# 32 affine and 12 weight-splitting operations move from GpSimd to VectorE, and the delta inverse's products skip zero and finished columns

## The chip, the cores and the metric

The kernel runs on one core of a Trainium2 chip. The metric is the device time of one execution in microseconds, as the median of several runs. The engines have short names here: PE is the matrix engine TensorE (PEld its loads of the stationary operand), DVE is VectorE, ACT is ScalarE, POOL is GpSimd, SP is SyncE, which issues most of the DMAs.

## The reference, cut to what matters

Two layers work on 256 latent and 256 context tokens of 1024 columns. Each layer is a SwiGLU FFN, a mixer and another FFN, and each of the three is closed by `x <- LN(alpha*x + gate*f(modulate(x)))`. The layer norm ends in an affine step:

```python
def layer_norm(x, g, b):
    mu = jnp.mean(x32, axis=-1, keepdims=True)
    var = jnp.mean(jnp.square(x32 - mu), axis=-1, keepdims=True)
    return ((x32 - mu) * lax.rsqrt(var + NORM_EPS) * g + b).astype(x.dtype)
```

The first layer's mixer is a windowed attention with 8 heads beside a gated delta rule in two directions with 4 heads, which needs the inverses of triangular matrices (one plus a strictly triangular part) over chunks of tokens. The second layer's mixer is a dense attention with normed and rotated queries and keys.

## The kernel before, in words

All tensors are float32. A product is made of three matmuls on halves: every weight tile of 128 x 1024 is split into a high part `wh` (ACT, L366) and a low part `wl = wr - wh` (DVE, or POOL where `split_w` is given that engine, L368); activations likewise into `ht_hi` (L261, L266) and `ht_lo` (L268). `mm3` (L383 to L386) multiplies high by high, high by low and low by high. Raw weight tiles `wr` have two buffers, and SP loads them in order.

An FFN runs over 22 chunks of 128 hidden columns in three parts (8, 8, 6). A chunk is 48 matmuls into `pgu` (gate and up); `evac` then makes `sg = silu(gate)` on ACT (L431), `sg * up` on DVE (L432), and splits it (L433, L434). `next_fill` hangs other DVE work behind each chunk, four additions of 1024 columns (L169) for the next modulation vector. After a part, the down products `pdn` are added to the residual rows `r` with the gate (L615, L623).

Between two sublayers stands `boundary(sub)`: `norm_tb` normalises four row blocks of 128 tokens, they are transposed, modulated and split as operands of the next sublayer, and `affine_tb` (L323 to L328) multiplies each row block by the norm's `g` (L326) and adds its `b` (L328). The operands don't need that affine step, since modulation contains it; the rows `r` need it before the next down products are added. For sub 3 it is deferred: `mixer_c` calls it in its scores loop at i = 4.

The first mixer (`ab_proj`) runs from about 415 to 500 us of the profile. It projects 13 chunks of 128 columns, with a convolution along tokens on DVE (`cacc`, L908), gates in small operations, and a DMA issued by POOL that stores the rows as `xs`. POOL then makes products of squares `sqT` (L1122). `delta_inverse` (584 to 634) interleaves with the window attention. For each of 8 units (4 tiles of 128 x 128) it forms a transposed `z`, the product `pN` (L1390), copies it to `va` (ACT, L1394), and three times makes a product `pZ` (L1403) and `o = xT - pZ` on DVE (L1408). Diagonal 32 x 32 blocks `xv` come by DMAs that SP and POOL issue (L1377). The window attention keeps POOL with products `qs` (L1290) that follow ACT.

The second mixer (`mixer_c`) projects from 1480 to 1557: products `pct`, statistics `cst`, normed rows `cx` (L1668), rotation (L1677 to L1681), transposes `pcT` (L1707) with their split `kTlo` (L1712). Its scores loop of 19 iterations follows to 1597 (scores `pSc`, maxima L1754, exponentials `cpe`, weights L1759), then down products, the leading chunks of the last FFN (`plead`, `ht_lo` L299), and that FFN.

A scheduler decides the order on each engine from a simulated timeline of its own. The code's order and explicit dependences (`after`) set what it may choose. Each engine then takes its instructions strictly in that order.

Of the kernel before, what the change touches and what calls it, by code (L numbers as in the profile page):

```python
# [10 lines left out]
F32 = mybir.dt.float32  # L11
F32R = mybir.dt.float32r
AF = mybir.ActivationFunctionType
# [19 lines left out]
class Backbone:  # L33
    def __init__(self, ctx, tc, io):
# [10 lines left out]
        self.lat_tags = LAT_TAGS  # L45
        self.turn_at = 0

    def new_ht(self):
# [274 lines left out]
    def affine_tb(self, tb, after):  # L323
        nc = self.nc
        x = self.row_block(tb)
        i = nc.gpsimd.tensor_tensor(out=x, in0=x, in1=self.lnr[:, 0, :], op=ALU.mult)  # L326
        self.after(i, [after])
        nc.gpsimd.tensor_tensor(out=x, in0=x, in1=self.lnr[:, 1, :], op=ALU.add)  # L328

# [68 lines left out]
    def ffn(self, sub, tail, lat_only=False, fill=()):  # L398
# [30 lines left out]
        def evac(c, pts):  # L429
            sg = fp.tile([128, NT], F32, tag="sg", name="sg", bufs=2)  # L430
            nc.scalar.activation(out=sg, in_=pts[0][:, :NT], func=AF.Silu)  # L431
            nc.vector.tensor_tensor(out=sg, in0=sg, in1=pts[1][:, :NT], op=ALU.mult)  # L432
            nc.scalar.activation(out=h_hi[:, c, :], in_=sg, func=AF.Copy)  # L433
            self.evacuated = nc.vector.tensor_tensor(out=h_lo[:, c, :], in0=sg, in1=h_hi[:, c, :].bitcast(F32), op=ALU.subtract)  # L434
            self.next_fill()

        parts = ((0, 8), (8, 16), (16, 22))
# [39 lines left out]
    def lead_weights(self, sub):  # L477
# [4 lines left out]
        for x in range(2):  # L482
# [6 lines left out]
            for y in range(2):  # L489
                hv, lv = self.split_w(t[:, 2 * y:2 * y + 2, :], x == 0, self.nc.gpsimd if x else None)  # L490
                ws += [(hv[:, z, :], lv[:, z, :]) for z in range(2)]
# [145 lines left out]
    def boundary(self, sub, streams=(0, 1), affine=(0, 1)):  # L637
# [6 lines left out]
        def rows(last):  # L644
            self.load_ln(sub)

            def apply():
                for j in affine:
                    for tb in (2 * j, 2 * j + 1):
                        self.affine_tb(tb, last)  # L650

            if sub == 3:
                self.deferred = apply
            else:
                apply()

# [235 lines left out]
    def ab_conv(self, pt, ch, dst, hold=(), aside=()):  # L892
# [7 lines left out]
        for j in (0, 1, 3, 4):  # L900
            o = j - 2
            t0, t1 = max(0, -o), LAT - max(0, o)
            if j in aside:
# [3 lines left out]
                continue  # L907
            nc.vector.scalar_tensor_tensor(  # L908
                out=av[:, :, t0:t1], in0=pv[:, :, t0 + o:t1 + o], scalar=w(j), in1=av[:, :, t0:t1],
# [26 lines left out]
    def ab_proj(self):  # L936
# [20 lines left out]
        def need(n):  # L957
            while len(ws) <= min(n, len(jobs) - 1):
# [5 lines left out]
                if p not in raws:  # L964
                    raws.clear()
                    raws[p] = self.load_w(w[:, :, p:p + 256])
                eng = nc.gpsimd if c0 < 1280 else None
                ws.append(self.split_w(raws[p][:, :, c0 - p:c0 - p + P], bool(ext), eng))
            return ws[min(n, len(jobs) - 1)]
# [25 lines left out]
        self.start_context()  # L995
        for j in range(2):
            nc.gpsimd.dma_start(out=self.xs[:, 2 * j:2 * j + 2], in_=self.rows[j])
        for n in range(4):
# [3 lines left out]
            if n:  # L1002
                k_tok(n - 1)
        self.vt = vt = L.tile([P, 4, 4, P], F32, tag="gate", name="vt", bufs=1)
        project(*need(4))
# [6 lines left out]
        for h in range(4):  # L1012
# [12 lines left out]
            if h == 1:  # L1025
                rows()

        for h in range(4):
# [6 lines left out]
            if h == 0:  # L1035
                q_tok(3)
                V.tensor_scalar(out=ssq, in0=ssq, scalar1=EPS, scalar2=None, op0=ALU.add)
                exps()
            self.ab_gram(h)
        self.ab_pow(self.rq, ssq, -0.5)  # L1040
        V.tensor_scalar(out=self.rq, in0=self.rq, scalar1=float(P) ** -0.5, scalar2=None, op0=ALU.mult)
# [319 lines left out]
    def delta_inverse(self):  # L1361
# [19 lines left out]
        def begin(n):  # L1381
# [4 lines left out]
            bt = cube(bt)  # L1386
            xT, x = (a, bt) if u < 4 else (bt, a)
            pN = self.bank("sc", "pN")
            for tb in range(4):
                nc.tensor.matmul(  # L1390
                    out=pN[:, tb * P:(tb + 1) * P], lhsT=self.AT[u][:, tb, :], rhs=x[:, tb, :], start=True, stop=True
                )
            N = self.tmp("va")
            i = nc.scalar.activation(out=N, in_=pN, func=AF.Copy)  # L1394
            if n == 7:
                self.mark = i
            state[n] = (xT, N, xT)

        def step(n, it):
            xT, N, Z = state[n]  # L1400
            pZ = self.bank("sc", "pZ")
            for tb in range(4):
                nc.tensor.matmul(  # L1403
                    out=pZ[:, tb * P:(tb + 1) * P], lhsT=N[:, tb * P:(tb + 1) * P], rhs=Z[:, tb, :],
                    start=True, stop=True,
                )
            Zn = self.AT[units[n]] if it == 2 else cube(self.tmp("o"))
            V.tensor_tensor(out=Zn, in0=xT, in1=cube(pZ), op=ALU.subtract)  # L1408
            state[n] = (xT, N, Zn)

# [221 lines left out]
    def mixer_c(self):  # L1632
# [53 lines left out]
        def weights(p):  # L1686
            raw = self.load_w(w[:, :, 256 * p:256 * p + 256])
            return [self.split_w(raw[:, 4 * x:4 * x + 4, :], p % 3 > 0, nc.gpsimd if x else None) for x in range(2)]

# [59 lines left out]
        def scores(i):  # L1749
# [8 lines left out]
            V.reciprocal(out=st[:, 3:4], in_=st[:, 2:3])  # L1758
            V.tensor_scalar(out=pe, in0=pe, scalar1=st[:, 3:4], scalar2=None, op0=ALU.mult)  # L1759
            state[i] = pe  # L1760
# [18 lines left out]
        for i in range(19):  # L1779
            if i == 4:  # L1780
                self.deferred()
            for n in (0, 1) if i == 0 else (i + 1,):
# [106 lines left out]
```

## Time and profile before

| | us |
|---|---|
| median of 3 runs | 1825.21 |
| lowest, highest | 1824.44, 1827.54 |
| profiled execution | 1826.35 |
| its span | 1824.6 |

The profile is of one execution. Its mean granted clock of PE is 0.987. A view that groups instructions gives their number, the time they were busy, the mean of one and the idle time just before them with what ended it. The timeline merges neighbours of one kind into a row with a count; the durations of neighbours overlap a little at their ends, so a row's time is a bit less than the sum of its members'. The waits count only time in which an engine stood idle for the named operation. A window lists for each engine the busy time and, in brackets, the instructions that touch it; the clock is the share of full speed granted to PE, and half of it is the lower of the clock's two levels.

### The profile page before, as it was taken

Reading aid. Unit: us, or ns where it says so; the run is one execution under the profiler, and the core shown is the slowest. Engines: PE = TensorE matmul, PEld = TensorE weight load, DVE = VectorE, ACT = ScalarE, POOL = GpSimd, SP = SyncE. Lnnn points to the kernel's source line nnn. Section 1 sums busy time; section 2 is a strip of 40 time slices with the busy share of each in tenths; the row PEclk is TensorE's granted clock in tenths of the full one; section 3 lists DMA queues with packets and bytes.
Section 4 is the critical chain, followed back from the end, with each engine's and each line's share of the span. In section 5 each row is a group of like instructions: output and inputs, shape, how many; then the busy total and the mean of one; then the engine's idle time right before and its main releaser. Section 6 shows DMA issues by size and latency. Waiting matters only on the chain. (4 is left out here: it accounts for less than half of the span.)

```text
span 1824.6 us, 24388 instructions
## 1 busy us (share of the span) xinstructions
PE 1758.4 (96%) x9571; PEld 1484.9 (81%) x9571; DVE 1264.7 (69%) x1912; ACT 672.8 (37%) x1178; POOL 290.7 (16%) x324
## 2 busy tenths in 40 slices
PE   6999999999998999999999999999999999999997
PEld 2978878878787888877887888778878888878997
DVE  2774855867688986896673438976747769786556
ACT  2432331324664662332221323423332335634442
POOL 1000000017433210510000003400000046150000
PEclk8999999999998999999999999999999999999999
DMA  9563553522341213375552242664644433136552
GB/s 349 185 216 128 185 182 120 197 59 95 127 116 54 75 59 104 128 240 187 162 184 70 93 154 77 212 204 141 204 163 139 155 108 113 59 126 232 186 177 99
DMA packets 178173, 267.56 MB, mean 147 GB/s; under 512 B 14639, under 2 KB 126683, under 8 KB 177547
## 3 DMA queue, kind: packets, MB, share of 16 engines
q1 hardware_dynamic: 172944, 250.58, 41.4%
q0 software_dynamic: 4624, 14.29, 2.4%
q8 instruction: 75, 1.23, 0.3%
q10 hardware_dynamic: 491, 1.15, 0.2%
q14 instruction: 39, 0.32, 0.1%
HBM read 259.64 MB, written 6.34 MB: 146 GB/s over the span
## 5 line engine op out<-in xcount | busy, mean ns | idle before, releaser
L366 ACT ACTIVATE wh<-wr 128x1024 fp32r<-128x1024 f32 (+1 forms) x311 | 324.8, 1056 | 756.7 <-PE pdn L386 306.6
L368 DVE TENSOR_TENSOR wl<-wr,wh 128x1024 fp32r<-128x1024 f32 (+1 forms) x299 | 390.0, 1315 | 231.9 <-ACT wh L366 228.5
L383 PE MATMUL pgu<-ht_hi,wh 128*128 128x512 f32 (+1 forms) x1472 | 519.5, 355 | 14.7 <-DVE sg L432 8.4
L386 PE MATMUL pgu<-ht_hi,wl 128*128 128x512 f32 (+1 forms) x1472 | 520.4, 354 | 3.3 <-DVE wl L368 3.3
L385 PE MATMUL pgu<-ht_lo,wh 128*128 128x512 f32 (+1 forms) x1472 | 520.6, 355 | 1.0 <-POOL ht_lo L268 0.5
L383 PEld LDWEIGHTS pgu<-ht_hi,wh 128*128 128x128 f32 x1472 | 279.1, 191 | 57.8 <-DVE sg L432 10.9
L386 PEld LDWEIGHTS pgu<-ht_hi,wl 128*128 128x128 f32 x1472 | 280.4, 191 | 41.6 <-DVE wl L368 3.9
L385 PEld LDWEIGHTS pgu<-ht_lo,wh 128*128 128x128 f32 x1472 | 280.5, 191 | 39.1 <-POOL ht_lo L268 0.9
L169 DVE SCALAR_TENSOR_TENSOR acc<-wa,cv,acc 128x1024 f32<-128x1024 f32 x224 | 277.1, 1299 | 0.0
L385 PE MATMUL pdn<-wl,hhi 128*128 128x512 f32 (+1 forms) x622 | 241.1, 388 | 0.0
L383 PE MATMUL pdn<-wh,hhi 128*128 128x512 f32 (+1 forms) x622 | 239.9, 389 | 0.0
L386 PE MATMUL pdn<-wh,hlo 128*128 128x512 f32 (+1 forms) x622 | 239.6, 388 | 0.0
L383 PEld LDWEIGHTS pdn<-wh,hhi 128*128 128x128 f32 x622 | 116.7, 188 | 27.6 <-issue 2.5
L385 PEld LDWEIGHTS pdn<-wl,hhi 128*128 128x128 f32 x622 | 116.9, 188 | 23.7
L386 PEld LDWEIGHTS pdn<-wh,hlo 128*128 128x128 f32 x622 | 116.9, 188 | 23.6
L432 DVE TENSOR_TENSOR sg<-sg,pgu 128x512 f32<-128x512 f32 (+1 forms) x86 | 53.6, 623 | 108.6 <-PE pgu L386 105.1
L615 DVE SCALAR_TENSOR_TENSOR tm<-pdn,gate 128x512 f32<-128x512 f32 (+1 forms) x98 | 64.3, 675 | 60.0 <-PE pdn L386 59.8
L197 POOL DMA_DIRECT2D gsc<-rows x12 | 6.2, 525 | 615.3 <-DVE rows L180 615.3
L433 ACT ACTIVATE hhi<-sg 128x512 fp32r<-128x512 f32 (+1 forms) x86 | 49.7, 577 | 89.4 <-DVE sg L432 89.3
L431 ACT ACTIVATE sg<-pgu 128x512 f32<-128x512 f32 (+1 forms) x86 | 45.9, 534 | 59.6 <-PE pgu L386 59.6
L434 DVE TENSOR_TENSOR hlo<-sg,hhi 128x512 fp32r<-128x512 f32 (+1 forms) x86 | 59.8, 695 | 7.7 <-ACT hhi L433 7.7
L318 POOL TENSOR_TENSOR mv<-mv,mhalf 128x1 f32<-128x1 f32 x18 | 16.6, 932 | 272.3 <-DVE mv L317 272.3
(385 smaller groups left out, 2351.3 us busy)
## 6 DMA issues: line engine op xcount, KB each, us to landing
wr<-in_ffn_w_gu_dram SPq DMA_DIRECT2D x84, 1024.0 KB
wa<-in_ada_w_dram SPq DMA_DIRECT2D x144, 512.0 KB
wr<-in_ffn_w_down_dram SPq DMA_DIRECT2D x40, 1024.0 KB
wr<-in_ab_w_in_dram SPq DMA_DIRECT2D x11, 1024.0 KB
wr<-in_c_w_in_dram SPq DMA_DIRECT2D x6, 1024.0 KB
gate<-gsc POOLq DMA_DIRECT2D x10, 512.0 KB, 4.5
wr<-in_ffn_w_gu_dram SPq DMA_DIRECT2D x8, 512.0 KB
wr<-in_ffn_w_down_dram SPq DMA_DIRECT2D x8, 512.0 KB
```

The source lines that it names most:

```text
L169: i = nc.vector.scalar_tensor_tensor(out=acc[:, sl], in0=wa[:, sl], scalar=cv, in1=acc[:, sl], op0=ALU.mult, op1=ALU.add)
L318: nc.gpsimd.tensor_tensor(out=mv[:, 3:4], in0=mv[:, 2:3], in1=self.mhalf[:, 0:1], op=ALU.pow)
L366: self.last_high = nc.scalar.activation(out=hv, in_=raw, func=AF.Copy)
L368: self.last_split = (eng or nc.vector).tensor_tensor(out=lv, in0=raw, in1=hv.bitcast(F32), op=ALU.subtract)
L383: self.first_mm = nc.tensor.matmul(out=out, lhsT=lhs[0], rhs=rhs[0], start=start, stop=False)
L385: self.link(nc.tensor.matmul(out=out, lhsT=lhs[0], rhs=rhs[1], start=False, stop=False))
L386: self.last_mm = nc.tensor.matmul(out=out, lhsT=lhs[1], rhs=rhs[0], start=False, stop=stop)
L431: nc.scalar.activation(out=sg, in_=pts[0][:, :NT], func=AF.Silu)
L432: nc.vector.tensor_tensor(out=sg, in0=sg, in1=pts[1][:, :NT], op=ALU.mult)
L433: nc.scalar.activation(out=h_hi[:, c, :], in_=sg, func=AF.Copy)
L434: self.evacuated = nc.vector.tensor_tensor(out=h_lo[:, c, :], in0=sg, in1=h_hi[:, c, :].bitcast(F32), op=ALU.subtract)
L615: i = nc.vector.scalar_tensor_tensor(out=tm, in0=pt[:, cs], scalar=mul, in1=self.gate[:, t // 2, ds], op0=ALU.mult, op1=ALU.mult)
```

## The change

1. Affine steps. `affine_tb` no longer issues anything. It puts a multiplication and an addition per row block on a list, and `next_affine` takes them from it one by one and issues them on DVE: two after the evacuation of chunks 2 to 5 of an FFN's first part, two behind the convolution of each of the four query heads in `ab_proj`, one in each of the iterations 2 to 5 of `mixer_c`'s scores loop. These are 8 + 8 operations ahead of FFNs two and three, 8 in `ab_proj`, 4 in the scores loop and 4 in the last FFN's leading chunks. The DMA that stores `xs` moves behind the affine operations of heads 1 and 3.
2. Splits. The 12 weight splits that `split_w` gave to POOL go to DVE: four of `ab_proj`, six of `mixer_c`, two of the last FFN's leading weights.
3. The inverse. Its matrices are triangular in blocks of 32 columns. `pN` is made for 96 instead of 128 columns, and of the three `pZ` the first has 96, the second 64 and the third 32. The subtraction covers these columns only and writes straight into `AT`. For each unit POOL gets a memset of the 32 columns of `va` that were not computed and a copy of 32 finished columns into `AT`.
4. `vt` is allocated after the first call of `ab_gram`.

```diff
     def affine_tb(self, tb, after):
         nc = self.nc
         x = self.row_block(tb)
-        i = nc.gpsimd.tensor_tensor(out=x, in0=x, in1=self.lnr[:, 0, :], op=ALU.mult)
-        self.after(i, [after])
-        nc.gpsimd.tensor_tensor(out=x, in0=x, in1=self.lnr[:, 1, :], op=ALU.add)
+        lnr = self.lnr
+
+        self.affine += [
+            lambda i=i: nc.vector.tensor_tensor(out=x, in0=x, in1=lnr[:, i, :], op=(ALU.mult, ALU.add)[i]) for i in range(2)
+        ]
+
+    def next_affine(self, n, behind):
+
+        for _ in range(min(n, len(self.affine))):
+            self.after(self.affine.pop(0)(), [behind])
...
             self.next_fill()
+            if n == 0 and c > 1:
+                self.next_affine(2, self.evacuated)
...
-                hv, lv = self.split_w(t[:, 2 * y:2 * y + 2, :], x == 0, self.nc.gpsimd if x else None)
+                hv, lv = self.split_w(t[:, 2 * y:2 * y + 2, :], x == 0)
...
-                eng = nc.gpsimd if c0 < 1280 else None
-                ws.append(self.split_w(raws[p][:, :, c0 - p:c0 - p + P], bool(ext), eng))
+                ws.append(self.split_w(raws[p][:, :, c0 - p:c0 - p + P], bool(ext)))
...
-        for j in range(2):
-            nc.gpsimd.dma_start(out=self.xs[:, 2 * j:2 * j + 2], in_=self.rows[j])
...
+            self.next_affine(2, self.convolved)
+            if h % 2:
+                nc.gpsimd.dma_start(out=self.xs[:, h - 1:h + 1], in_=self.rows[h // 2])
...
+            c0 = 0 if u < 4 else 32
             pN = self.bank("sc", "pN")
+            p3 = pN[:, 0:384].rearrange("p (t x) -> p t x", t=4)
             for tb in range(4):
                 nc.tensor.matmul(
-                    out=pN[:, tb * P:(tb + 1) * P], lhsT=self.AT[u][:, tb, :], rhs=x[:, tb, :], start=True, stop=True
-                )
-            N = self.tmp("va")
-            i = nc.scalar.activation(out=N, in_=pN, func=AF.Copy)
+                    out=p3[:, tb, :], lhsT=self.AT[u][:, tb, :], rhs=x[:, tb, c0:c0 + 96], start=True, stop=True
+                )
+
+            N = cube(self.tmp("va"))
+            i = nc.scalar.activation(out=N[:, :, c0:c0 + 96], in_=p3, func=AF.Copy)
+            zc = 96 if u < 4 else 0
+            nc.gpsimd.memset(N[:, :, zc:zc + 32], 0.0)
...
+            dc = 0 if u < 4 else 96
+            nc.gpsimd.tensor_copy(out=self.AT[u][:, :, dc:dc + 32], in_=xT[:, :, dc:dc + 32])
+            state[n] = (xT, N)
 
         def step(n, it):
-            xT, N, Z = state[n]
+
+            u = units[n]
+            xT, N = state[n]
+            w = 96 - 32 * it
+            c0 = 128 - w if u < 4 else 0
+            Z = xT if it == 0 else self.AT[u]
             pZ = self.bank("sc", "pZ")
+            p3 = pZ[:, 0:4 * w].rearrange("p (t x) -> p t x", t=4)
             for tb in range(4):
                 nc.tensor.matmul(
...
-            Zn = self.AT[units[n]] if it == 2 else cube(self.tmp("o"))
-            V.tensor_tensor(out=Zn, in0=xT, in1=cube(pZ), op=ALU.subtract)
-            state[n] = (xT, N, Zn)
+                    out=p3[:, tb, :], lhsT=N[:, tb, :], rhs=Z[:, tb, c0:c0 + w], start=True, stop=True,
+                )
+            V.tensor_tensor(
+                out=self.AT[u][:, :, c0:c0 + w], in0=xT[:, :, c0:c0 + w], in1=p3, op=ALU.subtract
+            )
...
-            return [self.split_w(raw[:, 4 * x:4 * x + 4, :], p % 3 > 0, nc.gpsimd if x else None) for x in range(2)]
+            return [self.split_w(raw[:, 4 * x:4 * x + 4, :], p % 3 > 0) for x in range(2)]
...
-            if i == 4:
-                self.deferred()
+            if 1 < i < 6:
+                self.next_affine(1, self.weighted)
```

How the order on the engines changes is shown at three places. In the changed kernel the lines are some 8 to 20 higher: L326 and L328 become L330, L368 L376, L432 L440, L434 L442, L169 L170, L615 L625, L623 L633, L1664 L1683, L1668 L1687, L1677 L1696, L1680 and L1681 L1699 and L1700, L1290 L1295, L1377 L1382, L1403 L1423.

First, DVE in the first part of the second FFN (third and fourth chunk); `acc` is the modulation vector, `r_6318` the latent rows. Before:

```order
L368 TENSOR_TENSOR wl<-wr,wh 128x1024 x2
L434 TENSOR_TENSOR hlo<-sg,hhi 128x512
L169 SCALAR_TENSOR_TENSOR acc_6923<-wa,cv,acc_6923 128x1024 x2
L169 SCALAR_TENSOR_TENSOR acc_6924<-wa,cv,acc_6924 128x1024 x2
L432 TENSOR_TENSOR sg<-sg,pgu_7108 128x512
L368 TENSOR_TENSOR wl<-wr,wh 128x1024
L434 TENSOR_TENSOR hlo<-sg,hhi 128x512
L169 SCALAR_TENSOR_TENSOR acc_6923<-wa,cv,acc_6923 128x1024 x2
```

and now:

```order
L376 TENSOR_TENSOR wl<-wr,wh 128x1024 x2
L330 TENSOR_TENSOR r_6318<-r_6318,lnr 128x1024
L442 TENSOR_TENSOR hlo<-sg,hhi 128x512
L170 SCALAR_TENSOR_TENSOR acc_6915<-wa,cv,acc_6915 128x1024 x2
L170 SCALAR_TENSOR_TENSOR acc_6916<-wa,cv,acc_6916 128x1024 x2
L330 TENSOR_TENSOR r_6318<-r_6318,lnr 128x1024
L440 TENSOR_TENSOR sg<-sg,pgu_7104 128x512
L376 TENSOR_TENSOR wl<-wr,wh 128x1024 x2
```

An affine operation now stands behind the two splits of a chunk, and a second one behind the additions, ahead of the next `sg`.

Second, DVE at the start of the second mixer, between the last additions to the rows and the first rotated `cx`. Before:

```order
L368 TENSOR_TENSOR wl<-wr,wh 128x1024
L623 TENSOR_TENSOR r_6319<-r_6319,tm 128x512 x2
L615 SCALAR_TENSOR_TENSOR tm<-pdn_11790,gate 128x512
L615 SCALAR_TENSOR_TENSOR tm<-pdn_11791,gate 128x512
L623 TENSOR_TENSOR r_6319<-r_6319,tm 128x512 x2
L1664 TENSOR_SCALAR cst<-cst 128x2
L1668 TENSOR_TENSOR cx<-pct,cst 128x256
L1677 TENSOR_TENSOR ct<-cx,tabc 128x256 x2
L368 TENSOR_TENSOR wl<-wr,wh 128x1024
L1680 TENSOR_TENSOR cx<-ct 128x2x64
L1681 TENSOR_TENSOR cx<-ct 128x2x64
```

and now:

```order
L376 TENSOR_TENSOR wl<-wr,wh 128x1024
L633 TENSOR_TENSOR r_6319<-r_6319,tm 128x512 x2
L376 TENSOR_TENSOR wl<-wr,wh 128x1024
L625 SCALAR_TENSOR_TENSOR tm<-pdn_11790,gate 128x512
L625 SCALAR_TENSOR_TENSOR tm<-pdn_11791,gate 128x512
L633 TENSOR_TENSOR r_6319<-r_6319,tm 128x512 x2
L1683 TENSOR_SCALAR cst<-cst 128x2
L1687 TENSOR_TENSOR cx<-pct,cst 128x256
L1696 TENSOR_TENSOR ct<-cx,tabc 128x256 x2
L376 TENSOR_TENSOR wl<-wr,wh 128x1024
L1699 TENSOR_TENSOR cx<-ct 128x2x64
L1700 TENSOR_TENSOR cx<-ct 128x2x64
```

A second split stands between the additions to the rows (and one more ahead of this piece), where POOL made it before; the rotation's own order is unchanged.

Third, POOL in the inverse. `qs` are products of the window attention, `xv` the diagonal blocks, `va` the copy of `pN`. Before:

```order
L1368 MEMSET xv 128x2048
L1290 TENSOR_TENSOR qs<-qTa,qs 64x128 x3
L1377 DMA xv<-scr_in 32x4x32 x8
L1290 TENSOR_TENSOR qs<-qTa,qs 64x128 x3
L1377 DMA xv<-scr_in 32x4x32 x2
L1290 TENSOR_TENSOR qs<-qTa,qs 64x128 x3
```

and now:

```order
L1373 MEMSET xv 128x2048
L1405 MEMSET va 128x4x32
L1295 TENSOR_TENSOR qs<-qTa,qs 64x128 x3
L1382 DMA xv<-scr_in 32x4x32 x8
L1295 TENSOR_TENSOR qs<-qTa,qs 64x128 x3
L1410 COPY AT<-xv 128x4x32
L1405 MEMSET va 128x4x32
L1382 DMA xv<-scr_in 32x4x32
L1410 COPY AT<-z 128x4x32
L1382 DMA xv<-scr_in 32x4x32
```

The memsets of `va` and the copies into `AT` stand among the `qs` and the issues of `xv` DMAs.

## Rows read from the trace of the kernel before

**Rows 1.** The page's shares: busy us, share of the span, instructions of each engine
```profile
PE 1758.4 (96%) x9571; PEld 1484.9 (81%) x9571; DVE 1264.7 (69%) x1912; ACT 672.8 (37%) x1178; POOL 290.7 (16%) x324
```

**Rows 2.** Groups of POOL: line, operation, shapes, count, busy us, mean ns, idle before
```profile
L328 POOL TENSOR_TENSOR r<-r,lnr 128x1024 f32<-128x1024 f32 x16 | 46.9, 2947 | 0.0
L326 POOL TENSOR_TENSOR r<-r,lnr 128x1024 f32<-128x1024 f32 x16 | 42.9, 2709 | 0.0
L368 POOL TENSOR_TENSOR wl<-wr,wh 128x1024 fp32r<-128x1024 f32 x12 | 29.9, 2497 | 11.5 <-ACT wh L366 11.5
```

**Rows 3.** Timeline of POOL behind the first mixer: start, us, operation, count
```profile
759.68 11.68 POOL L326 TENSOR_TENSOR r<-r,lnr 128x1024 f32<-128x1024 f32 x4
```

**Rows 4.** Timeline of DVE there, beside POOL and after it
```profile
762.34 10.10 DVE L368 TENSOR_TENSOR wl<-wr,wh 128x1024 fp32r<-128x1024 f32 x3
772.97 2.81 DVE L368 TENSOR_TENSOR wl<-wr,wh 128x1024 fp32r<-128x1024 f32 x1
...
806.35 2.36 DVE L368 TENSOR_TENSOR wl<-wr,wh 128x1024 fp32r<-128x1024 f32 x2
809.23 4.87 DVE L169 SCALAR_TENSOR_TENSOR acc<-wa,cv,acc 128x1024 f32<-128x1024 f32 x4
```

**Rows 5.** Waits of PE, 740 to 1210: us in total, times, longest
```profile
PE pgu L383 <- DVE sg L432: 8.4, 6, 2.0
```

**Rows 6.** Windows: length, busy us of PE, PEld, DVE, ACT, POOL, clock, DMA share, GB/s
```profile
440.00:485.00 45.00, 40.74 (x205) 31.74 (x204) 35.88 (x68) 28.03 (x87) 28.98 (x15) 0.96 0.34 117
584.00:634.00 50.00, 48.81 (x399) 45.07 (x399) 43.24 (x132) 30.22 (x99) 14.76 (x31) 0.94 0.22 69
800.00:820.00 20.00, 18.13 (x76) 14.54 (x76) 20.00 (x21) 7.08 (x9) 0.00 (x0) 0.95 0.76 254
...
880.00:890.00 10.00, 10.00 (x46) 8.29 (x45) 7.70 (x11) 2.12 (x2) 0.00 (x0) 1.00 0.27 94
...
1510.00:1540.00 30.00, 29.46 (x221) 28.32 (x220) 26.69 (x71) 17.26 (x53) 16.99 (x16) 0.91 0.41 141
1557.00:1580.00 23.00, 21.74 (x146) 18.58 (x145) 19.85 (x71) 18.32 (x55) 0.00 (x0) 1.00 0.07 24
```

**Rows 7.** Timeline of DVE at the second mixer's start
```profile
1492.63 2.51 DVE L268 TENSOR_TENSOR ht_lo<-h,ht_hi 128x256 fp32r<-128x256 f32 x1
...
1497.46 3.21 DVE L368 TENSOR_TENSOR wl<-wr,wh 128x1024 fp32r<-128x1024 f32 x1
...
1505.65 2.46 DVE L1677 TENSOR_TENSOR ct<-cx,tabc 128x256 f32<-128x256 f32 x2
...
1539.19 1.29 DVE L1677 TENSOR_TENSOR ct<-cx,tabc 128x256 f32<-128x256 f32 x2
```

**Rows 8.** Waits of PE, 1500 to 1560
```profile
PE pcT L1707 <- DVE cx L1681: 3.6, 1, 3.6
PE pcT L1707 <- DVE kTlo L1712: 2.0, 1, 2.0
```

**Rows 9.** Waits of PE, 1600 to 1660
```profile
PE pgu L386 <- DVE wl L368: 3.1, 2, 2.3
```

**Rows 10.** Timeline of DVE at the last FFN's start; in brackets idle time before
```profile
1629.86 10.02 DVE L368 TENSOR_TENSOR wl<-wr,wh 128x1024 fp32r<-128x1024 f32 x3
...
1648.14 1.23 DVE L368 TENSOR_TENSOR wl<-wr,wh 128x1024 fp32r<-128x1024 f32 x1 [5.22 <-ACT wh L366]
```

**Rows 11.** Timeline of PE: the inverse, and two passes of 32 moving columns
```profile
608.55 1.06 PE L1390 MATMUL pN<-z,AT 128*128 128x128 f32 x8
609.44 0.38 PE L1324 MATMUL pP<-ident,pexp 128*128 128x128 f32 x2
...
477.73 0.39 PE L859 MATMUL pgc<-gg,ones 128*128 128x32 f32 x2
```

**Rows 12.** Groups of lines in the inverse's stretch, 584 to 634
```profile
L1408 DVE TENSOR_TENSOR o<-xv,pZ 128x512 f32<-128x512 f32 x8 | 5.5, 683 | 3.1 <-PE pZ L1403 2.9
...
L1290 POOL TENSOR_TENSOR qs<-qTa,qs 64x128 fp32r<-64x128 f32 x20 | 9.2, 462 | 27.5 <-ACT qs L1289 27.2
```

More of the change, by code (lines that the diff above doesn't have):

```diff
@@ L46, in __init__ @@
         self.turn_at = 0
+        self.affine = []
     def new_ht(self):
@@ L645, in rows @@
             self.load_ln(sub)
[L647 to L655, printed above, removed]
+            for j in affine:
+                for tb in (2 * j, 2 * j + 1):
+                    self.affine_tb(tb, last)
         def context():
@@ L907, in ab_conv @@
                 continue
-            nc.vector.scalar_tensor_tensor(
+            self.convolved = nc.vector.scalar_tensor_tensor(
                 out=av[:, :, t0:t1], in0=pv[:, :, t0 + o:t1 + o], scalar=w(j), in1=av[:, :, t0:t1],
@@ L1003, in ab_proj @@
                 k_tok(n - 1)
-        self.vt = vt = L.tile([P, 4, 4, P], F32, tag="gate", name="vt", bufs=1)
         project(*need(4))
@@ L1039, in ab_proj @@
             self.ab_gram(h)
+            if h == 0:
+                self.vt = L.tile([P, 4, 4, P], F32, tag="gate", name="vt", bufs=1)
         self.ab_pow(self.rq, ssq, -0.5)
@@ L1387, in begin @@
             xT, x = (a, bt) if u < 4 else (bt, a)
+            c0 = 0 if u < 4 else 32
             pN = self.bank("sc", "pN")
+            p3 = pN[:, 0:384].rearrange("p (t x) -> p t x", t=4)
             for tb in range(4):
                 nc.tensor.matmul(
-                    out=pN[:, tb * P:(tb + 1) * P], lhsT=self.AT[u][:, tb, :], rhs=x[:, tb, :], start=True, stop=True
+                    out=p3[:, tb, :], lhsT=self.AT[u][:, tb, :], rhs=x[:, tb, c0:c0 + 96], start=True, stop=True
                 )
-            N = self.tmp("va")
-            i = nc.scalar.activation(out=N, in_=pN, func=AF.Copy)
+            N = cube(self.tmp("va"))
+            i = nc.scalar.activation(out=N[:, :, c0:c0 + 96], in_=p3, func=AF.Copy)
+            zc = 96 if u < 4 else 0
+            nc.gpsimd.memset(N[:, :, zc:zc + 32], 0.0)
             if n == 7:
                 self.mark = i
-            state[n] = (xT, N, xT)
+            dc = 0 if u < 4 else 96
+            nc.gpsimd.tensor_copy(out=self.AT[u][:, :, dc:dc + 32], in_=xT[:, :, dc:dc + 32])
+            state[n] = (xT, N)
         def step(n, it):
-            xT, N, Z = state[n]
+            u = units[n]
[3 more added lines that the diff above has]
+            Z = xT if it == 0 else self.AT[u]
             pZ = self.bank("sc", "pZ")
+            p3 = pZ[:, 0:4 * w].rearrange("p (t x) -> p t x", t=4)
             for tb in range(4):
                 nc.tensor.matmul(
-                    out=pZ[:, tb * P:(tb + 1) * P], lhsT=N[:, tb * P:(tb + 1) * P], rhs=Z[:, tb, :],
-                    start=True, stop=True,
-                )
-            Zn = self.AT[units[n]] if it == 2 else cube(self.tmp("o"))
-            V.tensor_tensor(out=Zn, in0=xT, in1=cube(pZ), op=ALU.subtract)
-            state[n] = (xT, N, Zn)
+                    out=p3[:, tb, :], lhsT=N[:, tb, :], rhs=Z[:, tb, c0:c0 + w], start=True, stop=True,
+                )
+            V.tensor_tensor(
+                out=self.AT[u][:, :, c0:c0 + w], in0=xT[:, :, c0:c0 + w], in1=p3, op=ALU.subtract
+            )
         jobs = []
@@ L1758, in scores @@
             V.reciprocal(out=st[:, 3:4], in_=st[:, 2:3])
-            V.tensor_scalar(out=pe, in0=pe, scalar1=st[:, 3:4], scalar2=None, op0=ALU.mult)
+            self.weighted = V.tensor_scalar(out=pe, in0=pe, scalar1=st[:, 3:4], scalar2=None, op0=ALU.mult)
             state[i] = pe
```

## The prediction

> **What bounds the kernel now.** I read the shares of the engines first: PE is busy 1758.4 of 1824.6 us, 96%, DVE 69%, POOL 16% [rows 1]. So the end is set by PE's work, plus 66 us in which PE stands still, plus what PE loses while its clock is granted low. A change of POOL and DVE work can win only there, and it loses wherever DVE comes later than PE.
>
> Second, POOL's operations of 1024 columns [rows 2]: 32 affine operations, 16 of 2.95 us and 16 of 2.71, and 12 splits of weights of 2.50: 46.9 + 42.9 + 29.9 = 119.7 us.
>
> Third, what stands beside them. At 759.68 POOL begins eight affine operations, the first four taking 11.68 us [rows 3]. At 762.34 DVE begins three splits that take 10.10 us, 3.37 each, and a fourth at 772.97 takes 2.81. Later, with POOL idle, two splits take 2.36 us and four additions of L169 4.87 [rows 4]. I take 1.2 us as the price of a 1024-column operation on an undisturbed DVE. So the two engines slow each other down: three splits cost DVE 10.10 us instead of 3.5.
>
> Fourth, where PE waits. Behind the two boundaries ahead of the second and third FFN it waits six times for `sg` (L432), 8.4 us [rows 5]. Around the second mixer's projections it waits 3.6 us for `cx` and 2.0 us for `kTlo` [rows 8], and ahead of the last FFN 3.1 us for `wl` [rows 9].
>
> **The change, part by part.** All sums are against the profiled execution: span 1824.6 plus 1.75 around it, 1826.35 us, which lies 1.1 above the median 1825.21. DVE takes on 44 operations of 1.2 us, 53 us in all. What that costs depends on the stage.
>
> *Boundaries ahead of the second and third FFN.* At each, eight affine operations leave POOL. DVE gets back 10.10 - 3.5 = 6.6 us on three splits and 2.81 - 1.2 = 1.6 on the fourth [rows 4], 8.2 us before the third chunk. It takes on 8 x 1.2 = 9.6 us, two operations in each of chunks 2 to 5. Such a chunk is sg 0.7, two splits 2.4, hlo 0.7 (bounded by a split of twice its columns), four additions 4.9 [rows 4], 8.6 us, and with two affine operations 11.0 by full durations; with the overlap that the starts show (two splits in 2.36) nearer to 10.6. PE needs 48 matmuls: 46 touch the 10 us from 880 to 890, so about (10 + 0.4)/46 = 0.226 us each and 10.8 a chunk [rows 6]. DVE is then full, but in four chunks only, and without a backlog from before them. In the kernel before it is the backlog that makes sg late: in 800 to 820 DVE is busy all 20.00 us, PE 18.13 [rows 6]. I expect the waits to go, 4.2 us at each boundary. At 800 to 820 the clock is also 0.95, 0.05 x 20 = 1 us. I take -5 for the first boundary (ends -2 and -5.2) and -3.5 for the second (-1 and -4.2), which leaves a little for the full chunks.
>
> *First mixer's projections (440 to 485).* Eight affine operations (9.6 us) and four splits (4.8) come to DVE, which has 45.00 - 35.88 = 9.1 us free [rows 6]. 14.4 against 9.1: if nothing is given back, 5.3 us stick out. Some of DVE's 35.88 is slowed by POOL, busy 28.98 us there; if that gives back 5.3, the cost is nothing. Ends 0 and +5.3; I take +1.5, nearer to nothing, since the boundaries show what POOL's company costs DVE [rows 4]. The store of `xs`, a DMA that POOL issues, comes later and now waits for DVE's last affine operation; behind it in POOL's queue stand rq and the products of squares (L1122). They would be late if DVE reached that operation only after 485, so I cost the move at nothing with +1 as its upper end, inside the +5.3.
>
> *The inverse's columns (584 to 634).* Moving columns fall from 128 to 96 in pN, and to 96, 64 and 32 in the three products pZ. A group of eight passes begins at 608.55 and the next stretch of work at 609.44: 0.89/8 = 0.111 us for 128 moving columns. Two passes with 32 moving columns and the same stationary size take 0.39 together [rows 11]; as one alone lasts about 0.28 (1.06 less seven pitches), their pitch is 0.11 as well. So the pitch doesn't follow the moving columns here, and PE gains nothing from fewer. DVE's 24 subtractions (0.683 us for 512 columns [rows 12]) lose a quarter, a half and three quarters of their columns: at most 8 x 0.683 x 1.5 = 8.2 us, off the path except where PE waits. PE idles 50.00 - 48.81 = 1.2 us in this stretch [rows 6], which bounds that gain. POOL gets a memset and a copy for each of 8 units, at some 0.46 us (the nearest row, L1290 [rows 12]) 7.4 us in a stretch where it is busy 14.76 of 50: hidden, but for the case of rival C. I take -1, ends -1.2 and +2.
>
> The Trainium skill, "TensorE: Matmul & The Clock Gate", section "LDWEIGHTS (loading the stationary operand)", says that loading the stationary operand takes time by its own columns, about P/1.2 ns: an estimate of 107 ns for 128. By that rule fewer moving columns gain nothing and the sum stands; the trace's 0.111 us agrees. The page's section "Back-to-back issue gap" has the gap of an isolated matmul fall with its moving columns; by that the sum would be rival A's.
>
> *Start of the second mixer.* At 1492.63 an ht_lo of 256 columns takes 2.51 us, at 1497.46 a split 3.21, and at 1505.65 two L1677 take 2.46, which at 1539.19 take 1.29 [rows 7]. DVE wins at least 1.3 + 2.0 + 1.2 = 4.5 us; two more splits ahead of the first L1664 take 2.4 of it. So `cx` comes 2.1 to 2.5 us earlier, of a wait of 3.6 [rows 8]. Behind that gap the clock is 0.91 in 1510 to 1540, 0.09 x 30 = 2.7 us [rows 6]; I count 1. Together -3.5, ends 0 and -6.3. The 2.0 us for `kTlo` go with the POOL work beside them: -2, ends 0 and -2.
>
> *Scores loop (1557 to 1597).* Four affine operations, 4.8 us, go where DVE is busy 19.85 and PE 21.74 of 23.00 us [rows 6]. DVE's free 3.15 us lie in small pieces. Ends 0 and +4.8; I take +2.5.
>
> *Lead and last FFN.* Three splits at 1629.86 took 10.02 us beside POOL; alone they take 3.5. PE's 3.1 us for `wl` should go [rows 9]. The four affine operations stand where DVE had a hole of 5.22 us ahead of 1648.14 [rows 10], so I cost them at nothing; should the hole close, they would cost up to 4.8 of DVE. -3, ends +1 and -6.
>
> **The sum:** -5 - 3.5 + 1.5 - 1 - 3.5 - 2 + 2.5 - 3 = -14.0. 1826.35 - 14.0 = 1812.35, and on the scale of the median, 1.1 less, 1811.
>
> **Rivals.** *A: PE's time follows the columns in the inverse.* 64 passes of pN lose 32 columns each, 64 of each pZ lose 32, 64 and 96: 64 x 224 = 14,336 columns at 0.111/128 us are 12.4 us. For it: no row shows a long run of passes with 32 to 96 columns. Against it: the pair with 32 [rows 11]. It gives 1799. Chance 0.10.
>
> *B: DVE takes POOL's place and the gains are given back.* The boundaries give -1 each because a full DVE leaves no room, the mixer's start 0, kTlo -2, the lead -3, the inverse 0, while the first mixer and the scores loop cost +5.3 and +4.8: +3.1, that is 1828; with half of those two costs, 1823. For it: DVE's 35.88 of 45 and 19.85 of 23 us [rows 6]. Against it: POOL's drag on DVE, 8.2 us at a boundary, is nearly as large as the work that moves, 9.6. Chance 0.13, nearly all of it within 0.2%.
>
> *C: slower, by POOL's queue in the inverse.* The first pZ of a unit now waits for POOL's memset of `va`, and in that queue stand qs (L1290), which waits for ACT 27.2 us over 20 operations, 1.4 each [rows 12], and the issues of xv. If each of the eight units pays one such wait, a qs, a copy and a memset, 1.4 + 3 x 0.46 = 2.8, then 22 us are on the path and the end is 1833. It decides from 18 us on, 2.2 a unit. For it: all of these stand in one queue, one behind the other. Against it: POOL is mostly idle there, and other products lie between. Chance 0.07.
>
> **How the numbers follow.** Forecast 0.70, A 0.10, B 0.13, C 0.07. About 0.2%, 3.65 us, is what a measurement of this kernel can tell: faster means under 1821.6, slower over 1828.9. Forecast and A are faster, 0.80; B the same, 0.13; C slower, 0.07. All better ends together give -24.9, all worse ones +10.1, and they won't all meet. Down I take two thirds of the 10.9 us between, 1811 - 7 = 1804, and 1801 for part of A. Up I take half of the 24.1, 1823, which holds the lower part of B; the worse ends of the first mixer and the scores loop need a DVE that gets nothing back, and those of the boundaries one that does.
>
> **What would show it.** Right: DVE's splits at 1.2 us all along, no wait for sg behind the boundaries, pZ passes still 0.11 us apart, the scores loop 2 to 3 us longer. Wrong: PE waiting for sg or the convolution from a DVE without gaps, pZ passes closer than 0.11 us, or PE waiting for `va` from POOL.

## The result and the profile after

The changed kernel takes 1802.35 us (median of 4 runs, 1800.41 to 1803.31) against 1825.97 for the kernel before: a ratio of 0.9869, 95% interval 0.9852 to 0.9886, 23.6 us faster. The forecast was 1811 within 1801 to 1823. The span fell from 1824.6 to 1800.3. The page's shares, as in [rows 1]:

```profile
PE 1757.1 (98%) x9571; PEld 1481.2 (82%) x9571; DVE 1239.4 (69%) x1956; ACT 670.4 (37%) x1176; POOL 180.5 (10%) x296
```

PE does the same work in 1.3 us less and now fills 98% of the span; POOL lost 110 us of work, and DVE, which took 44 operations on, is busy for 25 us less than before. Two groups of lines on DVE show part of it (line, operation, shapes, count, busy us, mean ns, idle before):

```profile
L376 DVE TENSOR_TENSOR wl<-wr,wh 128x1024 fp32r<-128x1024 f32 x310 | 375.3, 1222 | 220.8 <-ACT wh L374 217.3
...
L330 DVE TENSOR_TENSOR r<-r,lnr 128x1024 f32<-128x1024 f32 x32 | 39.0, 1218 | 0.0
```

The splits now take 1222 ns in the mean, the slowest 1228 (the 298 of before had a mean of 1319 and took up to 3.4 us), so 12 more of them cost 14 us less in total; the affine operations take 1218 ns each and add 39 us. The rest comes from other lines that also lost POOL's company, the splits of activations above all (`ht_lo` L268 from 31.9 to 21.3 us, `hlo` L434 from 51.3 to 45.2), and from the inverse's subtractions, which have fewer columns (16.4 to 10.0).

Where the time went is read from the start of the same instruction on DVE in both timelines, after less before, at the ends of six stages. The same was done for each experiment; the table has the change within a stage, in us, for the profiled execution.

| kernel | to the first mixer's last `tm` (744) | first boundary, to chunk 8 (897) | second FFN, second boundary, to chunk 8 (1272) | to the first score (1559) | scores, to the lead (1621) | last FFN (1798) | sum |
|---|---|---|---|---|---|---|---|
| changed | -0.8 | -6.8 | -2.7 | -5.9 | +1.2 | -9.3 | -24.3 |
| changed again | -2.6 | -6.8 | -2.7 | -6.1 | +1.2 | -9.5 | -26.5 |
| e1, affine only | +7.3 | -2.1 | -2.7 | -2.8 | +1.3 | -5.5 | -4.5 |
| e2, splits only | +3.7 | +1.5 | 0.0 | +1.9 | -0.1 | 0.0 | +7.0 |
| e3, inverse only | +3.0 | -2.0 | 0.0 | +0.1 | +1.9 | +0.5 | +3.5 |
| e4, affine on POOL | +7.4 | -0.1 | +3.7 | -7.1 | +2.8 | -1.5 | +5.2 |
| e5, no affine | -3.5 | -4.8 | -5.4 | -6.1 | -0.1 | -9.3 | -29.2 |
| e6, late in the scores | -2.0 | -6.7 | -2.7 | -6.2 | +0.6 | -9.2 | -26.2 |
| e7, last FFN only | +0.2 | 0.0 | 0.0 | 0.0 | 0.0 | -8.1 | -7.9 |
| e8, without the inverse | -0.3 | -2.3 | -2.7 | -6.2 | +1.2 | -8.3 | -18.6 |
| e9, boundaries only | +0.3 | -4.8 | -2.7 | -0.3 | -0.1 | +0.8 | -6.8 |
| e10, second mixer only | +0.1 | 0.0 | 0.0 | -7.6 | +1.4 | +4.0 | -2.1 |
| e11, first mixer only | 0.0 | +4.2 | 0.0 | +0.1 | -0.1 | +1.6 | +5.8 |

One execution of a kernel differs from the next: the two rows of the changed kernel by 2 us, mostly ahead of 744, and the 12 to 23 times of the kernel before on one chip by 7 to 9 us from lowest to highest. The table has one execution of each, against the profiled execution of the kernel before, so its sums differ from the medians below by up to 3.5 us. The executions of e1, e2, e3, e9, e10 and e11 in it lie 1 to 3 us above their medians.

**The first boundary.** DVE's timeline in the changed kernel, one full chunk (as [rows 4]), and its window (length, busy us of PE, PEld, DVE, ACT, POOL, clock, DMA share, GB/s; as in [rows 6]):

```profile
803.77 0.68 DVE L440 TENSOR_TENSOR sg<-sg,pgu 128x512 f32<-128x512 f32 x1
804.37 2.35 DVE L376 TENSOR_TENSOR wl<-wr,wh 128x1024 fp32r<-128x1024 f32 x2
806.64 1.22 DVE L330 TENSOR_TENSOR r<-r,lnr 128x1024 f32<-128x1024 f32 x1
807.77 0.69 DVE L442 TENSOR_TENSOR hlo<-sg,hhi 128x512 fp32r<-128x512 f32 x1
808.38 4.87 DVE L170 SCALAR_TENSOR_TENSOR acc<-wa,cv,acc 128x1024 f32<-128x1024 f32 x4
813.16 1.22 DVE L330 TENSOR_TENSOR r<-r,lnr 128x1024 f32<-128x1024 f32 x1
814.29 0.68 DVE L440 TENSOR_TENSOR sg<-sg,pgu 128x512 f32<-128x512 f32 x1
```

```profile
800.00:820.00 20.00, 20.00 (x90) 16.57 (x89) 20.00 (x20) 6.49 (x8) 0.00 (x0) 1.00 0.64 213
```

Splits, affine operations and additions follow each other at 1.13 to 1.2 us. From one `sg` (803.77) to the next (814.29) are 10.52 us, and DVE has no gap, but PE has none either. Where it waited 8.4 us for `sg` over both boundaries [rows 5], there is now no such wait.

**The last FFN.** Timeline of DVE and windows (to be read beside [rows 10]):

```profile
1612.60 3.50 DVE L376 TENSOR_TENSOR wl<-wr,wh 128x1024 fp32r<-128x1024 f32 x3 [0.39 <-ACT wh L374]
...
1621.45 1.22 DVE L330 TENSOR_TENSOR r<-r,lnr 128x1024 f32<-128x1024 f32 x1
```

```profile
1620.00:1640.00 20.00, 15.86 (x83) 12.59 (x81) 17.29 (x19) 8.52 (x16) 14.35 (x10) 0.91 0.12 38
1640.00:1665.00 25.00, 22.34 (x178) 21.54 (x179) 12.02 (x17) 10.10 (x15) 0.00 (x0) 1.00 0.73 245
```

```profile
1605.00:1620.00 15.00, 14.81 (x92) 12.29 (x91) 9.52 (x20) 8.92 (x17) 1.81 (x4) 1.00 0.23 70
1620.00:1641.00 21.00, 20.88 (x175) 20.68 (x174) 16.29 (x20) 10.52 (x15) 0.58 (x1) 1.00 0.73 246
```

The first pair of windows is the kernel before, the second the changed one. Before, PE stood still for 4.1 and 2.7 us there, and its clock was 0.91 in the first of them; now for 0.2 and 0.1, at full clock.

**The inverse.** Timeline of PE (as [rows 11]):

```profile
612.92 1.02 PE L1423 MATMUL pZ<-z,va 128*128 128x96 f32 x8
613.78 1.03 PE L1423 MATMUL pZ<-AT,va 128*128 128x64 f32 x8
614.65 0.39 PE L1329 MATMUL pP<-ident,pexp 128*128 128x128 f32 x2
...
615.90 1.00 PE L1423 MATMUL pZ<-AT,va 128*128 128x64 f32 x8
616.73 0.39 PE L1329 MATMUL pP<-ident,pexp 128*128 128x128 f32 x2
616.96 0.98 PE L1423 MATMUL pZ<-AT,va 128*128 128x32 f32 x8
617.77 0.71 PE L1303 MATMUL pS<-kk,qs 128*128 128x512 f32 x2
```

Eight passes of 96 moving columns take 0.86 us to the next start, of 64 columns 0.83 (615.90 to 616.73), of 32 columns 0.81 (616.96 to 617.77), and before 0.89 for 128: 0.108, 0.104 and 0.101 us a pass against 0.111.

### The profile page after: what moved, and what is told of

Same layout as the page of the kernel before. It is cut to its first block, busy times and chain, and to the rows that moved or that the text cites. A ratio compares the mean times of both kernels' runs of the same rounds, so it can differ in the third digit from the quotient of the medians.

```text
span 1800.3 us, 24410 instructions
## 1 busy us (share of the span) xinstructions
PE 1757.1 (98%) x9571; PEld 1481.2 (82%) x9571; DVE 1239.4 (69%) x1956; ACT 670.4 (37%) x1176; POOL 180.5 (10%) x296
## 5 line engine op out<-in xcount | busy, mean ns | idle before, releaser
L376 DVE TENSOR_TENSOR wl<-wr,wh 128x1024 fp32r<-128x1024 f32 (+1 forms) x311 | 375.5, 1219 | 220.8 <-ACT wh L374 217.3
L170 DVE SCALAR_TENSOR_TENSOR acc<-wa,cv,acc 128x1024 f32<-128x1024 f32 x224 | 272.8, 1279 | 0.0
L440 DVE TENSOR_TENSOR sg<-sg,pgu 128x512 f32<-128x512 f32 (+1 forms) x86 | 53.6, 623 | 109.0 <-PE pgu L394 105.0
L625 DVE SCALAR_TENSOR_TENSOR tm<-pdn,gate 128x512 f32<-128x512 f32 (+1 forms) x98 | 64.3, 675 | 61.2 <-PE pdn L394 61.1
L442 DVE TENSOR_TENSOR hlo<-sg,hhi 128x512 fp32r<-128x512 f32 (+1 forms) x86 | 53.6, 624 | 12.2 <-ACT hhi L441 12.2
L394 PE MATMUL pproj<-ht_hi,wl 128*128 128x512 f32 (+1 forms) x160 | 56.1, 355 | 0.0
```

Source lines behind the costliest of these rows:

```text
L170: i = nc.vector.scalar_tensor_tensor(out=acc[:, sl], in0=wa[:, sl], scalar=cv, in1=acc[:, sl], op0=ALU.mult, op1=ALU.add)
L376: self.last_split = (eng or nc.vector).tensor_tensor(out=lv, in0=raw, in1=hv.bitcast(F32), op=ALU.subtract)
L394: self.last_mm = nc.tensor.matmul(out=out, lhsT=lhs[1], rhs=rhs[0], start=False, stop=stop)
L625: i = nc.vector.scalar_tensor_tensor(out=tm, in0=pt[:, cs], scalar=mul, in1=self.gate[:, t // 2, ds], op0=ALU.mult, op1=ALU.mult)
```

## The experiments

The first four take the change apart by its parts.

**e1_affine_only**: the changed kernel with the inverse of before and with the 12 splits back on POOL.

```diff
-                hv, lv = self.split_w(t[:, 2 * y:2 * y + 2, :], x == 0)
+                hv, lv = self.split_w(t[:, 2 * y:2 * y + 2, :], x == 0, self.nc.gpsimd if x else None)
```

> The affine steps go to VectorE at the places of the changed kernel; the 12 splits stay on GpSimd and the inverse stays as before. Theory (the gain is GpSimd's affine work no longer slowing VectorE): the changed kernel gained 6.7 us at the first boundary, 2.7 at the second, 9.4 around the last FFN's start and lost about 2 in the scores loop; all of that belongs to the affine steps, and about half of the 5.9 at the second mixer. So -18 to -21 against the kernel before, near 1806. Rival (the gain is shared evenly by the three parts, or comes from the inverse): -8 to -12, near 1816.

Measured: 1819.37 against 1827.39, ratio 0.9951 (0.9935 to 0.9967), -8.0 us. The theory missed; the figure is the lower end of the rival's -8 to -12, but not for the rival's reason. The table puts the miss in the first mixer, where it is 7.3 us later. The waits of PE (580 to 640) and of ACT (560 to 592) in this run:

```profile
PE pS L1304 <- POOL qs L1296: 8.0, 1, 8.0
```

```profile
ACT qs L1295 <- DVE X L1182: 7.1, 1, 7.1
```

The chain: PE waits 8.0 us for `qs`, which waits for ACT, which waits for the last step of a serial solve on DVE (`X`). DVE's first operation on the gram matrices ahead of that solve came 7.0 us later than before and the last one 6.0 later. In the changed kernel the first came 3.3 later, but the last 0.5 earlier, and the solve began 0.5 earlier: there the rows of gram matrices themselves make up the delay, not the solve.

**e2_splits_only**: the kernel before, its 12 splits on DVE (the reverse of that diff, at three places).

> Only the 12 weight splits go to VectorE. Theory: they matter only where GpSimd made them, at the first mixer's projections (near 0) and at the start of the second mixer, where the wait for cx (3.6 us) shrinks by 2 to 4 us: -2 to -4 against the kernel before, near 1823. Rival (the two more splits ahead of the first statistics take back what the freed VectorE wins): 0 or slower, 1826 to 1829.

Measured: 1832.96, ratio 1.0030 (1.0019 to 1.0042), +5.6 us. The sign is the rival's, the place only in part. At the second mixer the first `cx` comes 2.1 us earlier, as the theory has it, but 4.0 us are lost again up to the first score, where the affine work is still on POOL and PE waits 2.4 us for an `ht_lo` of DVE; and the first mixer came 3.7 later.

**e3_inverse_only**: the kernel before with `begin` and `step` of the changed one.

> Only the inverse's products skip columns. Theory (a pass lasts as long as the load of its 128 stationary columns): passes of 96, 64 and 32 moving columns start 0.108, 0.104 and 0.101 us apart as in the changed kernel's trace, against 0.111 for 128, worth 1.6 us, so 0 to -2 against the kernel before, within 0.2% of it. Rival (time follows columns): -12, near 1814. Second rival (the memset and copy on GpSimd hold up the products): slower by 3 us or more.

Measured: 1828.13, ratio 1.0001 (0.9990 to 1.0012). As the theory has it; "time follows columns" (-12) is excluded, and so is the second rival's 3 us.

**e4_affine_pool**: the changed kernel with one word changed.

```diff
-            lambda i=i: nc.vector.tensor_tensor(out=x, in0=x, in1=lnr[:, i, :], op=(ALU.mult, ALU.add)[i]) for i in range(2)
+            lambda i=i: nc.gpsimd.tensor_tensor(out=x, in0=x, in1=lnr[:, i, :], op=(ALU.mult, ALU.add)[i]) for i in range(2)
```

> The changed kernel, but the affine steps, at the same places in the code, run on GpSimd. Theory (the engine matters, since the two engines slow each other): most of the gain of the boundaries and of the last FFN is lost, and the time is 1815 to 1822. Rival (the gain comes from spreading the affine steps over four chunks rather than from the engine): within 3 us of the changed kernel's 1802.

Measured: 1831.42, ratio 1.0025 (1.0015 to 1.0036): 29 us slower than the changed kernel and 9 beyond the theory's range, so the list without the other engine brings nothing. Whether spreading the operations matters on DVE stays open, since the planner put the eight operations in a row here. POOL's timeline, DVE's beside it, and PE's waits from 790 to 870:

```profile
765.18 24.00 POOL L330 TENSOR_TENSOR r<-r,lnr 128x1024 f32<-128x1024 f32 x8
...
767.86 10.09 DVE L376 TENSOR_TENSOR wl<-wr,wh 128x1024 fp32r<-128x1024 f32 x3
```

```profile
PE pgu L391 <- DVE sg L440: 5.7, 2, 3.7
```

It is the collision of [rows 3, 4] again: three splits in 10.09 us, and PE waits 5.7 us for `sg`.

The parts alone give -8.0 + 5.6 + 0.7 = -1.7 us and together -23.6, so they don't add. The next runs take the change apart by stages of the kernel.

**e7_last_only**, **e9_bounds_only**: the kernel before, with the list of affine operations for one place (e9: `sub in (1, 2)`).

```diff
-                        self.affine_tb(tb, last)
+                        self.affine_later(tb) if sub == 4 else self.affine_tb(tb, last)
```

> The kernel before, with only the four affine operations ahead of the last FFN on VectorE, in its leading chunks. It tells the local gain there from one that needs the rest of the change. Theory (GpSimd's affine work delays three splits of VectorE by 6.5 us, these delay the raw weight buffers and the next loads, and PE stands still behind them): the changed kernel's 9.3 us at this place, or the 6 us of the run with the affine part alone: -6 to -9.5, near 1819. Rival (only PE's wait for wl goes, 3.1 us): -3, near 1824.

> The kernel before, with only the affine operations ahead of the second and third FFN on VectorE, two behind each of chunks 2 to 5. Theory (the stages are independent of each other): the changed kernel's -6.8 and -3.1, so -9 to -10, near 1817. Rival (the first boundary's gain in the changed kernel came partly from the first mixer's end, since the affine part alone gained 2.1 there): -5, near 1822.

Measured: e7 1819.14 against 1826.88 (0.9955, 0.9939 to 0.9972), -7.7 us; e9 1818.39 (0.9950, 0.9935 to 0.9964), -8.5. Both are close to their theories, e9 half a microsecond short of its range. In e7 the trace is the same as before up to the lead, and then 8.1 us are won. The three splits of [rows 10] in e7, and the wait of SP's queue, which loads the weights, from 1612 to 1641, before and in e7:

```profile
1628.28 3.50 DVE L381 TENSOR_TENSOR wl<-wr,wh 128x1024 fp32r<-128x1024 f32 x3 [0.40 <-ACT wh L379]
```

```profile
SPq L336 <- DVE sg L507: 25.6, 1, 25.6
```

```profile
SPq L349 <- DVE sg L522: 17.5, 1, 17.5
```

The splits end at 1631.78 instead of 1639.88, 8.1 us earlier: they are 6.5 us shorter, and they begin 1.6 earlier, behind an `ht_lo` of 0.29 us instead of 2.37. The next load of weights, which in the program waits for the third of these splits, is held for 17.5 us instead of 25.6, which is 8.1 again (the view names the `sg` that DVE starts just as the splits end). So the theory's chain holds: late splits hold the raw buffers, and so the loads and PE. POOL's four operations there cost 8 us and not 3.

**e10_second_mixer_only**: six splits and the four deferred operations of the second mixer, as in the change.

> The kernel before, with only the second mixer changed: its six splits on VectorE and the four deferred affine operations in iterations 2 to 5 of the scores loop on VectorE. Theory (each of the two alone leaves the other to collide with VectorE, so both have to go): the changed kernel's -5.9 up to the scores and +1.5 to +2 in the loop, -4 in all, near 1823. Rival (their sum, each measured alone: -2.8 and +1.8 up to the scores): 0 to +1, near 1828.

Measured: 1822.26 (0.9969, 0.9956 to 0.9983), -4.6 us, as the theory has it. Up to the first score -7.6, more than in the changed kernel: either part alone gave -2.8 or +1.9. In the profiled execution, the slowest of nine, 4 us are lost again in the last FFN, where POOL's affine work still meets DVE's splits: PE waits 3.8 us for `wl` and 3.3 for `wh` there (3.3 and 1.4 before), and the clock is 0.91 and 0.93 in the two windows.

**e11_first_mixer_only**: its four splits, eight affine operations and the store of `xs`, as in the change; **e8_no_inverse**: the changed kernel with the inverse of before.

> The kernel before, with only the first mixer changed: its four splits and its eight affine operations on VectorE, the store of xs behind them, the inverse as before. Theory (each of the two alone came 6 to 7 us later at the first gram matrices, since VectorE and GpSimd still met there; together they come 3 later, and the solve behind has that much slack): -1 to +1 against the kernel before at the end of the inverse, within 0.2% at the end. Rival (VectorE is too full at this place): +4 to +7 at the end of the inverse, 1830 or more.

> The changed kernel with the inverse's products as before: affine steps and splits alone. Theory (a pass goes by its stationary columns): 0 to +2 against the changed kernel, 1802 to 1804. Rival (the column part is what the other two lack to add up, since the affine part alone gave 8 us, the splits alone lost 5, the inverse alone gave nothing, and all three give 23.6): +10 to +20, 1812 to 1822.

Measured: e11 1831.42 against 1827.81 (1.0020, 1.0010 to 1.0030), +3.6; e8 1808.06 (0.9889, 0.9874 to 0.9903), 6.1 above the changed kernel's 1801.92 of the same chip. Neither end is the theory's, though at the end of the inverse both are where the theory put them (0.0 and -0.4). What they lose comes behind it. Waits of PE from 640 to 770 in e8, and the window 745 to 770 in e8 and in the changed kernel:

```profile
PE pgu L391 <- DVE tm L625: 3.1, 1, 3.1
```

```profile
745.00:770.00 25.00, 24.73 (x190) 24.31 (x191) 16.07 (x29) 11.20 (x17) 4.69 (x7) 0.94 0.21 66
```

```profile
745.00:770.00 25.00, 24.72 (x181) 23.21 (x180) 17.30 (x31) 16.18 (x22) 4.41 (x6) 1.00 0.40 130
```

In the first chunk of the second FFN PE waits 3.1 us for `tm`, and the clock is 0.94 behind that gap (0.06 x 25 = 1.5 us). That is e8's whole loss at the first boundary, -2.3 against -6.8. In e11 the wait is 3.1 instead of 1.9, the clock behind it 0.93 instead of 1.00, and PE waits 6.1 us for `sg` from 770 to 910 instead of 4.5: 1.2 + 1.7 + 1.6 = 4.5, near its +4.2.

The instructions of PE and DVE stand there in the same order in the changed kernel and in e8. What differs is where the planner puts an accumulator. In all 13 kernels the second product of that chunk goes to bank 2 of the PSUM, the memory of PE's sums. The built programs show whose sums lie in that bank before, among the mixer's last two down products, which `tm` reads in turn:

| bank 2 holds | kernels | PE's wait for `tm` |
|---|---|---|
| the first of the two | before, e2, e7, e9, e10 | 1.9 us |
| the second | e1, e5, e8, e11 | 3.1 us |
| neither (they lie in banks 3 and 5) | changed, e3, e4, e6 | none |

So the wait follows the bank in every kernel. The inverse's new products lead the planner to the last row, except in e5. Why it does so, by a simulated timeline that shorter operations shift, is argued and not shown.

The last two ask what is left.

**e5_no_affine**: the changed kernel, in which `next_affine` only empties the list.

> The changed kernel with the affine steps left out (the rows are not multiplied by g nor is b added). What VectorE pays for the 32 operations. Theory (hidden at the boundaries and in the last FFN, 2 us in the scores loop, 1 to 3 in the first mixer): 2 to 5 us under the changed kernel's 1802, near 1798. Rival (VectorE is the bound in the full chunks): 8 us or more under it.

Measured: 1797.75 (0.9837, 0.9823 to 0.9852). That is 4 to 5 us under the changed kernel: 2.7 at the second boundary and 1.3 in the scores. The theory's figure came out partly by luck, since e5 has the wait for `tm`, which cost e8 4.5 us at the first boundary. Without it the gap would be some 9 us (an estimate from 4.2 and 4.5), the rival's figure. But the rival's reason is not seen at the second boundary: PE waits for nothing over 0.3 us there in either kernel. What differs is its own work. Sixteen small products `pada` for the modulation vector stand in four groups in the changed kernel and in one in e5 and in the kernel before. One of the four groups, and the one group of e5:

```profile
1208.84 1.05 PE L137 MATMUL pada<-acc,pick 128*32 128x512 f32 x4
```

```profile
1200.66 1.93 PE L137 MATMUL pada<-acc,pick 128*32 128x512 f32 x16
```

Up to the product behind each group the four take 3.96 us together, the one 1.88: 2.1 us of the 2.7. e8 and e9, which have the affine operations in these chunks, have the four groups at both boundaries too.

**e6_late_scores**: the four operations of the scores loop in its iterations 14 to 17.

```diff
-            if 1 < i < 6:
+            if 13 < i < 18:
```

> The changed kernel, with the four affine operations of the scores loop in its iterations 14 to 17, where VectorE has room, instead of 2 to 5. Theory (VectorE is the bound of the first half of that loop, which is 1.8 us longer in the changed kernel and 0.1 without the affine steps): 1.5 to 2 us under the changed kernel, near 1800.5, and the lead behind the loop not later. Rival (they are then late for the rows that the next products are added to): same as the changed kernel or 1 to 2 us slower.

Measured: 1801.81 against 1801.92 of **after_again**, the changed kernel on the same chip (ratios 0.9856 and 0.9859): no difference, as the rival has it. The loop wins 0.6 us to the lead, and nothing of it can be told at the end. No kernel that does the whole work beats the changed one.

> The changed kernel on the same chip, as the measure for the other three: 1802 to 1803, 23 to 24 under the kernel before.

## Why the prediction was right

The direction, the mechanism and the range held; the gain was 23.6 where the sum had 14.0 (14.2 on the medians). That the time lies in the range is in part luck: the lower end of 1801 had been 1804 without an allowance for rival A, which fell, and 1802.35 lies below 1804. Step by step, predicted and then as the table has it:

- **First boundary** -5: -6.8. The waits for `sg` went, as worked out, and DVE runs four full chunks without making PE wait. The sum left out the 1.9 us wait for `tm` in the FFN's first chunk. It stood in the trace and went too, but by the inverse's part: e3, which has nothing else of the change, gains 2.0 here, and e9, where that wait stays, gives -4.8.
- **Second boundary** -3.5: -2.7, in e9 as well. The waits gave more than the 4.2 worked out (e5: -5.4); the price was 2.7 and not the 0.7 that the sum left for full chunks, and 2.1 of it is the `pada` of PE, which the sum didn't have.
- **First mixer and inverse** +1.5 - 1 = +0.5: -0.8, within what one run differs from another. The first gram matrices do come 3.3 us later, and the later ones make it up. But the cover is thin: with half of the move (e1, e2) the first mixer ends 4 to 7 us later. The inverse's passes got 0.003 to 0.010 us shorter, 8 x 8 x (0.003 + 0.003 + 0.007 + 0.010) = 1.5 us where the sum had 1. By its own sign (passes closer than 0.11 us) the prediction was a little wrong here; rival A's 12 us fell with the pass of 32 columns, 0.101 us, and with e3. The Trainium skill, "TensorE: Matmul & The Clock Gate", section "LDWEIGHTS (loading the stationary operand)", gives the load of the stationary operand a time by its own columns, an estimate of 107 ns for 128. The trace's 0.111 to 0.101 us lie within 6% of it on either side, so it is near the pitch but not a floor under it.
- **Second mixer** -3.5 - 2 = -5.5: -5.9. The waits for `cx` and `kTlo` are gone.
- **Scores loop** +2.5: +1.2 to the lead, less than the 2 to 3 named as a sign.
- **Lead and last FFN** -3: -9.3. This is the term that was mis-sized. It counted the wait for `wl` [rows 9] alone. PE's idle time in 1620 to 1665 was 6.8 us, of which 3.3 under that name, 1.4 for `wh`, 1.0 for `ht_lo`, 0.7 for the rows and 0.3 for `sg`, and 0.09 x 20 = 1.8 us went to the clock. Together 8.6, and e7 gave 8.1: the whole stretch hung on the three splits and the load behind them.

Rival B (DVE takes POOL's place) is seen only in its ends: e5 puts the price of the 32 operations at 4 to 5 us, some 9 without its wait for `tm`. Rival C (POOL's queue in the inverse) did not come about: no product waits for `va` in the changed kernel, and e3 is not slower.

What was not on the list is that the parts need each other. The affine operations alone gave -8.0 and the splits alone +5.6, both together -19.8 (e8). By stages it comes nearer: -7.7 (e7), -8.5 (e9), -4.6 (e10), +3.6 (e11) and -6.1 (the inverse, changed kernel less e8) make -23.3, against 25.9 measured on that chip. That is no proof that stages add. The inverse is worth -6.1 only behind the rest of the change (e3 alone: +0.7, which would make -16.5), and place by place the four don't add: in the last FFN their rows sum to -1.7 us, where the changed kernel has -9.3.

## What to carry to other kernels

Where two engines slow each other, try moving all of the one's heavy work out of a stage before judging a part of the move: the two halves alone were worth -8 and +6 us, both together -20. Size a stall by the idle time and the clock of its whole stretch, not by the one wait whose name the change touches. And when a small edit in one stage seems to be worth six microseconds in the next, look for a wait there that comes and goes with the planner before crediting the edit; here the accumulator's bank told.

## What the runs showed of the hardware

- Both engines lose when POOL's affine operations meet DVE's splits. In e4 POOL takes 2.39 us for one with DVE idle (at 436 us) and 3.3 to 3.5 beside the splits; a split takes 3.36 beside it and 1.22 alone. Beside convolutions of DVE, which read `pproj` from the PSUM, POOL keeps its 2.4 us (before, 440 to 460).
- A pass with 32 moving columns is not quite as long as one with 128: 0.101 against 0.111 us, a small but steady slope.
- In e8 a gap of 3.1 us on PE cost about half as much again: the mean clock is 0.94 in the 25 us behind it, where the changed kernel has 1.00. A gap of 1.9 us at the same place had 1.00 behind it in the kernel before, e7, e9 and e10, and 0.93 in e2.
